# Another order for the mixers of the second block: differential maps, GLA and HGRN first, then NSA; levels later in priority

## The chip, the cores and the metric

The kernel runs on one core of a Trainium2 chip. The metric is the device time of one execution in microseconds (us), as a median of runs. The engines are PE (matrix products), DVE (vector), ACT (scalar functions), POOL (GpSimd) and SP (it issues the loads).

## The reference, cut to what matters

Two blocks of two layers each, 256 tokens, width 1024, all in float32. The change touches the attention part of the second block, which runs once a layer:

```python
for i in range(DEPTH):                      # 2 layers
    u = rms_norm_2(h, norm_attn[i]) @ w_in[i]          # 3228 columns, split
    o_a = nsa_attention(...)   # gates: compressed + selected + window attention
    o_b = diff_attention(...)  # softmax map 0 minus lambda times softmax map 1
    o_c = gla_mixer(...)       # gated linear attention, 4 heads, dk 32
    o_d = hgrn2_mixer(...)     # the same recurrence, forget gate f, 4 heads, dk 64
    h = h + jnp.concatenate([o_a, o_b, o_c, o_d], -1) @ w_out[i]
    ...                        # dense FFN (layer 0) or 8 experts (layer 1)

# NSA: hidden = silu(blocks of 32 tokens @ cmp_w1) ; kc, vc = hidden @ cmp_w2
#   o = g0 * attn(q, kc, vc) + g1 * attn(q, k_slc, v_slc) + g2 * attn(q, k_win, v_win)
# GLA and HGRN: S_t = diag(exp(log_g_t)) S_{t-1} + k_t v_t^T ;  o_t = S_t^T q_t
```

With 256 tokens every block is selected and every token lies in the window, so the selected and the window part are two causal maps with keys of their own.

## The kernel before, in words

A float32 product is computed as three products of split operands (`mm3`, lines 143 to 148: high x high, low x high, high x low). Weights are loaded 1024 rows deep by SP, split on ACT (`whi`, line 136) and DVE or POOL (`wlo`, line 139). `proj_tok` gives tokens on partitions (tile `pt`), `proj_ch` channels on partitions (tile `pc`).

Each layer runs `block2_mixers`. Its program has these parts, by the names in the profile:

- dqk projection: q and k of differential attention, squared and scaled, then transposed (`dqt`).
- nsa (512 columns) and nd (396 columns): NSA's q, k, v and gates, and the v of differential attention. From them NSA's keys and queries are normed (`nsq`, `nr`, `qn`) and transposed (`nqt`).
- `compressed()`: compressed attention of NSA, a serial chain: block sums (`zp`, `BT`), the product with cmp_w1 in two halves (`hp`, `ht`), then `kcp`, `kcs`, `kct`, `kbd`, `scp`, a softmax on 16 columns (`pcm`), `pct`, `pcT`, and `oc`.
- vr, rq, gqk: values, GLA's gate, queries, keys and forget gates. A scan along time gives the summed log gates (`gcat`), products of q and k on the diagonal give `dg`, and from it `AT` is started as a diagonal matrix.
- The levels: the decay between tokens i and j is split at seven block sizes (1 to 64). Each level computes `E` (DVE, then the exponential on ACT), `Kt` (POOL), `Qg` (DVE), two `Qh` (POOL), then the products `pg`, `ph` (PE), of which DVE (for the largest sizes ACT) copies a part into `AT`. An eighth one (`Ex`, `Ktx`, `Qgx`, `Qhx`, `pgx`, `phx`) covers the two halves of the sequence.
- The maps: softmax maps of NSA (`nl`, `npr`, `npt`, `npo`) and of differential attention (`dl`, `de`, `dpt`, `dpo`). `npt` is a transpose on PE, `nptT` its copy by ACT, and `npo` the product with the values, scaled into `mix` on DVE.
- og and rio: gates and HGRN's values, 256 and 512 columns.
- gpo (`AT` times values), the norm, the transposes of `mix` (`ptr`), and the out-projection (tiles `pt` on `xh`).

The order on each engine is made by a scheduler that simulates the program. Among the instructions that it takes to be ready it puts the one of smallest priority first; a priority is the place in the program, unless the program sets `tc.cur_priority`. Each engine then executes in that order. Before the change the program sets it three times: what follows the start of `compressed()` gets 3000 more, the rest of `compressed()` and all the maps get the smaller number back. PSUM tiles come from a pool with tags: "mx" (3 banks: maps), "gd" (2 banks: levels, `dg`, compressed attention, `gpo`) and "mm" (projections).

Of the kernel before, what the change touches and what calls it, by code (L numbers as in the profile page):

```python
# [10 lines left out]
F32 = mybir.dt.float32  # L11
# [1080 lines left out]
LEVELS = (1, 2, 4, 8, 16, 32, 64)  # L1092

# [84 lines left out]
def block2_mixers(k, a, l, hl, pre):  # L1178
# [5 lines left out]
    with ExitStack() as es:  # L1184
# [56 lines left out]
        proj_tok(k, w[:, 0:512], 512, hl, ev_n)  # L1241
        proj_tok(k, [w[:, 512:652], w[:, 1164:1420]], 396, hl, ev_nd)

        nr = one.tile([P, 2, 6], F32, name="nr")
        for tt in range(2):
            sq = n2("nsq")[:, :384].rearrange("p (g d) -> p g d", g=6)
            f = lambda s_, e_: nsa[:, tt, s_:e_].rearrange("p (g d) -> p g d", d=64)
            nc.gpsimd.tensor_tensor(sq[:, 0:4], f(0, 256), f(0, 256), op=ALU.mult)  # L1250
            nc.gpsimd.tensor_tensor(sq[:, 4:5], f(384, 448), f(384, 448), op=ALU.mult)
            nc.gpsimd.tensor_tensor(sq[:, 5:6], f(512, 576), f(512, 576), op=ALU.mult)
            nc.vector.tensor_reduce(nr[:, tt], sq, axis=AX.X, op=ALU.add)
        nrf = nr.rearrange("p t g -> p (t g)")
        nc.vector.tensor_scalar(nrf, nrf, 1.0 / 64, EPS, op0=ALU.mult, op1=ALU.add)
        powm(k, nrf, nrf, -0.5)
        qT = one.tile([P, 2, T], F32, name="nqT")
        kTs = one.tile([P, T], F32, name="nkTs")
        kTw = one.tile([P, T], F32, name="nkTw")
        for tt in range(2):  # L1260
            gain = lambda i: r2.nsa[:, 64 * i : 64 * i + 64]
            qn = n2("qn").rearrange("p (g d) -> p g d", d=64)
            for g in range(6):
                src = [0, 64, 128, 192, 384, 512][g]
                dst = qn[:, g if g < 5 else 6]
                nc.vector.scalar_tensor_tensor(dst, nsa[:, tt, src : src + 64], nr[:, tt, g : g + 1],
                                               gain(0 if g < 4 else g - 2), op0=ALU.mult, op1=ALU.mult)
            nc.gpsimd.tensor_copy(qn[:, 5], qn[:, 4])
            nc.gpsimd.tensor_copy(qn[:, 7], qn[:, 6])
            pt = pst("nqt")  # L1270
            for m in range(4):
                nc.tensor.transpose(pt[:, m * P : (m + 1) * P], qn[:, 2 * m : 2 * m + 2].rearrange("p g d -> p (g d)"),
                                    k.ident)
            sl = slice(tt * P, (tt + 1) * P)
            nc.scalar.copy(qT[:, :, sl], pt[:, :256].rearrange("p (m t) -> p m t", m=2))
            nc.scalar.copy(kTs[:, sl], pt[:, 256:384])
            nc.scalar.copy(kTw[:, sl], pt[:, 384:512])
# [5 lines left out]

        def compressed():
            zp = gdt("zp").rearrange("p (j n) -> p j n", j=4)[:, :2]
            selm = k.ident.rearrange("p (n two) -> p n two", two=2)
            for j in range(2):
                for par in range(2):
                    for tt in range(2):
                        nc.tensor.matmul(zp[64 * par : 64 * par + 64, j, tt * 64 : tt * 64 + 64],  # L1290
                                         nsa[:, tt, 256 + 64 * j : 320 + 64 * j], selm[:, :, par],
                                         start=True, stop=True)
            sel4 = one.tile([P, 32], F32, name="sel4")
            nc.vector.tensor_reduce(sel4, k.ident.rearrange("p (q n) -> p n q", q=4), axis=AX.X, op=ALU.add)
            zt = one.tile([P, 2, P], F32, name="zt")
            nc.vector.tensor_copy(zt, zp)

            BT = [n2("BT").rearrange("p (m n) -> p m n", m=16) for _ in range(2)]
            hid = one.tile([P, 2, 2, 15], F32, name="hid")
            w2c = one.tile([P, 2, 2, 64], F32, name="w2c")  # L1300
            nc.sync.dma_start(w2c, a["nsa_cmp_w2_2"][l].rearrange("j (b p) d -> p j b d", p=P))
            hr = one.tile([P, 2, 4, 16], F32, name="hr")
            nc.vector.memset(hr, 0.0)
            for j in range(2):
                nc.gpsimd.memset(BT[j], 0.0)
                z3 = zt[:, j].rearrange("p (n m) -> p n m", m=8)
                pos = k.pc[:, PC_POS + 32 * l + 16 * j : PC_POS + 32 * l + 16 * j + 16]
                for hf in range(2):
                    o = BT[j][:, 8 * hf : 8 * hf + 8, :15].rearrange("p m n -> p n m")
                    nc.vector.tensor_tensor(o, z3[:, hf : hf + 15, :],  # L1310
                                            pos[:, None, 8 * hf : 8 * hf + 8].to_broadcast([P, 15, 8]), op=ALU.add)
            yield
            for j in range(2):

                hp = gdt("hp")[:, :256]
                raws = [load_w(k, a["nsa_cmp_w1_2"][l, j, q * 1024 : (q + 1) * 1024, :], 256) for q in range(2)]
                for m in range(16):
                    nc.tensor.matmul(hp[32 * (m % 4) : 32 * (m % 4) + 32], BT[j][:, m], raws[m // 8][:, m % 8, :],
                                     start=m < 4, stop=m >= 12)
                hs = n2("chs")[:, :256]  # L1320
                nc.scalar.copy(hs, hp)
                yield

                ht = gdt("ht")[:, :32].rearrange("p (b n) -> p b n", b=2)
                for b in range(2):
                    nc.tensor.matmul(ht[:, b], hs[:, b * P : (b + 1) * P], sel4[:, :16], start=True, stop=True)
                th = n2("cth")[:, :32].rearrange("p (b n) -> p b n", b=2)
                nc.scalar.activation(th, ht, AF.Tanh, scale=0.5)
                nc.vector.scalar_tensor_tensor(th, th, 1.0, ht, op0=ALU.add, op1=ALU.mult)
                nc.vector.tensor_scalar(hid[:, j], th[:, :, :15], 0.5, None, op0=ALU.mult)  # L1330
                yield
            for b in range(2):
                nc.vector.tensor_copy(hr[:, b, :, 0:15], hid[:, 1, b : b + 1, :].to_broadcast([P, 4, 15]))
            kp = gdt("kcp")
            for b in range(2):
                nc.tensor.matmul(kp[:15, 0:64], hid[:, 0, b, :], w2c[:, 0, b, :], start=b == 0, stop=b == 1)
            for b in range(2):
                nc.tensor.matmul(kp[:64, 64:128], hr[:, b].rearrange("p h n -> p (h n)"), w2c[:, 1, b, :],
                                 start=b == 0, stop=b == 1)
            kcs = one.tile([P, 2, 64], F32, name="kcs")  # L1340
            nc.vector.memset(kcs[:16], 0.0)
            ks1 = one.tile([16, 1], F32, name="ks1")
            kj = one.tile([16, 64], F32, name="kj")
            nc.scalar.activation(kj[:15], kp[:15, 0:64], AF.Square, accum_out=ks1[:15])
            nc.vector.tensor_scalar(ks1[:15], ks1[:15], 1.0 / 64, EPS, op0=ALU.mult, op1=ALU.add)
            nc.gpsimd.tensor_tensor(ks1[:15], ks1[:15], k.pw[-0.5][:15, 0:1], op=ALU.pow)
            for j in range(2):
                nc.vector.scalar_tensor_tensor(kcs[:15, j, :], kp[:15, 0:64], ks1[:15], r2.nsa[:15, 64:128],
                                               op0=ALU.mult, op1=ALU.mult)
            vbd = one.tile([64, 4, 64], F32, name="vbd")  # L1350
            nc.vector.tensor_tensor(vbd, kp[:64, None, 64:128].to_broadcast([64, 4, 64]),
                                    c["bd16"][:64, :, None].to_broadcast([64, 4, 64]), op=ALU.mult)
            yield
            kct = gdt("kct")
            nc.tensor.transpose(kct[:, :16], kcs[:16].rearrange("p a d -> p (a d)"), k.ident[:16, :16])
            kbd = one.tile([P, 2, 16], F32, name="kbd")
            nc.vector.tensor_tensor(kbd, kct[:, None, :16].to_broadcast([P, 2, 16]),
                                    c["bd64"][:, :, None].to_broadcast([P, 2, 16]), op=ALU.mult)
            yield
            scp = gdt("scp")[:, :128].rearrange("p (t h n) -> p t h n", t=2, h=4)  # L1360
            for tt in range(2):
                for m in range(2):
                    nc.tensor.matmul(scp[:, tt, 2 * m : 2 * m + 2, :], qT[:, m, tt * P : (tt + 1) * P], kbd,
                                     start=True, stop=True)
# [762 lines left out]
```

## Time and profile before

| what | value |
| --- | --- |
| median of 3 runs | 2451.25 us (2448.11 to 2455.19) |
| profiled execution | 2451.29 us, its span 2449.2 us |
| mean granted clock of PE in the span | 0.981 |
| PE busy | 2355.3 us, 96% |
| DVE, ACT, POOL busy | 1905.5, 1469.9, 457.8 us |
| mixers of layer 0, dqk's tail to the out-projection | 722.5 to some 872 us of the span |

Times in the profile are microseconds from the span's start. A window's row gives its length, each engine's busy time with the number of instructions, the share of full clock that PE was granted, the share of the DMA engines and the rate. A timeline row joins neighbours of one form; its xN counts records, and PE's ends are modelled, so that neighbours overlap: the distance of two starts is what one costs.

### The profile page before, as it was taken

The page shows a single profiled execution, that of the slowest core. Times are in us where ns is not written, and L with a number is a line of the kernel's source. Part 1 is how long each engine was busy: PE and PEld are TensorE (multiplying, and loading weights), DVE is VectorE, ACT ScalarE, POOL GpSimd, SP SyncE. Part 2 cuts the span into 40 slices and gives each one's busy share as a digit, 9 for nine tenths or more (in the row PEclk, how much of TensorE's full clock was granted, in tenths as well). Part 3 has the DMA queues.
Part 4 walks back from the last instruction along what each step waited for, and adds up shares of the span by engine and source line. Part 5 has one row for each costly group of instructions (what it writes and reads, how often), then busy time and mean ns, then how long its engine had stood idle before and what let it go on. Part 6 is the DMA issues. An engine that isn't in the chain of part 4 may idle for free. (4 is left out here: it accounts for less than half of the span.)

```text
span 2449.2 us, 35398 instructions
## 1 busy us (share of the span) xinstructions
PE 2355.3 (96%) x13251; PEld 1972.1 (81%) x13251; DVE 1905.5 (78%) x2828; ACT 1469.9 (60%) x2239; POOL 457.8 (19%) x466
## 2 busy tenths in 40 slices
PE   8999999999999799999988999999999999999997
PEld 7898879888878589998776787887878787878785
DVE  5858576776766955556587799999999999998996
ACT  5455554455455444445454677777777777777774
POOL 3434114532133621111454100000000000000000
PEclk9999999999999799999997999999999999999999
DMA  7343254343345135465540999999999999999962
GB/s 245 105 138 121 87 168 156 122 137 121 130 158 173 39 129 196 166 206 192 160 143 5 360 367 332 355 346 342 344 345 344 342 345 343 345 343 345 344 255 87
DMA packets 288734, 550.07 MB, mean 225 GB/s; under 512 B 17414, under 2 KB 95020, under 8 KB 288300
## 3 DMA queue, kind: packets, MB, share of 16 engines
q1 hardware_dynamic: 287372, 546.67, 64.0%
q8 instruction: 106, 1.74, 0.3%
q0 software_dynamic: 144, 1.05, 0.1%
q14 instruction: 72, 0.59, 0.1%
q10 hardware_dynamic: 1040, 0.03, 0.0%
HBM read 545.61 MB, written 2.10 MB: 224 GB/s over the span
## 5 line engine op out<-in xcount | busy, mean ns | idle before, releaser
L139 DVE TENSOR_TENSOR wlo<-raw,whi 128x1024 fp32r<-128x1024 f32 x948 | 1159.9, 1240 | 294.8 <-ACT whi L136 285.8
L136 ACT CAST whi<-raw 128x1024 fp32r<-128x1024 f32 x984 | 1025.4, 1048 | 549.8 <-PE pt L147 92.1
L145 PE MATMUL pt<-whi,xh 128*128 128x512 f32 (+3 forms) x656 | 251.6, 396 | 14.6 <-DVE q L606 3.1
L146 PE MATMUL pt<-wlo,xh 128*128 128x512 f32 (+3 forms) x656 | 256.7, 392 | 2.9 <-DVE wlo L139 2.6
L147 PE MATMUL pt<-whi,xl 128*128 128x512 f32 (+3 forms) x656 | 253.2, 388 | 0.0
L237 POOL TENSOR_TENSOR nr<-nms,pwm 128x1 f32<-128x1 f32 x16 | 8.8, 549 | 1155.2 <-DVE nms L252 1155.2
L146 PE MATMUL ya<-wlo,hh 128*128 128x512 f32 x448 | 180.8, 404 | 0.0
L145 PE MATMUL mg<-whi,xg 128*128 128x512 f32 x448 | 180.4, 403 | 0.0
L146 PE MATMUL mg<-wlo,xg 128*128 128x512 f32 x448 | 178.0, 397 | 0.0
L147 PE MATMUL mg<-whi,xg 128*128 128x512 f32 x448 | 176.8, 395 | 0.0
L145 PE MATMUL mu<-whi,xg 128*128 128x512 f32 x448 | 176.8, 395 | 0.0
L146 PE MATMUL mu<-wlo,xg 128*128 128x512 f32 x448 | 176.7, 394 | 0.0
L147 PE MATMUL ya<-whi,hl 128*128 128x512 f32 x448 | 176.6, 395 | 0.0
L147 PE MATMUL mu<-whi,xg 128*128 128x512 f32 x448 | 176.6, 394 | 0.0
L145 PEld LDWEIGHTS pt<-whi,xh 128*128 128x128 f32 x656 | 125.0, 192 | 40.3 <-issue 8.8
L145 PE MATMUL pc<-xh,whi 128*128 128x256 f32 (+1 forms) x496 | 145.2, 293 | 6.5 <-DVE q L605 2.2
L146 PEld LDWEIGHTS pt<-wlo,xh 128*128 128x128 f32 x656 | 125.7, 192 | 28.9 <-DVE wlo L139 6.2
L146 PE MATMUL pc<-xl,whi 128*128 128x256 f32 (+1 forms) x496 | 143.9, 290 | 0.0
L147 PEld LDWEIGHTS pt<-whi,xl 128*128 128x128 f32 x656 | 125.6, 192 | 22.6 <-DVE xl L278 1.1
L147 PE MATMUL pc<-xh,wlo 128*128 128x256 f32 (+1 forms) x496 | 143.7, 290 | 0.0
L145 PE MATMUL ya<-whi,hh 128*128 128x512 f32 x448 | 140.8, 395 | 0.0
L145 PE MATMUL gu<-xh,whi 128*128 128x256 f32 x448 | 126.7, 283 | 0.0
(638 smaller groups left out, 4795.1 us busy)
## 6 DMA issues: line engine op xcount, KB each, us to landing
raw<-in_moe_w_gate SPq DMA_DIRECT2D x112, 1024.0 KB, 5.6
raw<-in_moe_w_up SPq DMA_DIRECT2D x112, 1024.0 KB, 5.3
raw<-in_moe_w_down SPq DMA_DIRECT2D x112, 1024.0 KB, 5.4
raw<-in_w_in SPq DMA_DIRECT2D x92, 1024.0 KB, 5.2
raw<-in_w_out SPq DMA_DIRECT2D x16, 1024.0 KB, 5.0
raw<-in_ffn_w_gate SPq DMA_DIRECT2D x14, 1024.0 KB, 5.2
raw<-in_ffn_w_up SPq DMA_DIRECT2D x14, 1024.0 KB, 5.3
raw<-in_ffn_w_down SPq DMA_DIRECT2D x14, 1024.0 KB, 5.6
```

The lines of the kernel that those rows point to most:

```text
L136: nc.scalar.copy(hi, raw_view)
L139: k.last_split = eng.tensor_sub(lo, raw_view, hi)
L145: nc.tensor.matmul(out, lh, rh, start=start, stop=False)
L146: nc.tensor.matmul(out, lh, rl, start=False, stop=False)
L147: return nc.tensor.matmul(out, ll, rh, start=False, stop=stop)
L237: return k.nc.gpsimd.tensor_tensor(out, in_, k.pw[e][:, :n], op=ALU.pow)
```

## The change

The parts of `block2_mixers` stand in another order. Differential maps come right behind the gates, alone; then vr, GLA's gate, rq, gqk, the scan, `dg` and the start of `AT`; then the nsa projection with its preparation; then `compressed()` and the NSA maps in turns; then the levels, og, rio and the rest. In place of the settings of `tc.cur_priority` there is one addition of 3000 ahead of the levels, never taken back. `compressed()` takes its PSUM tiles from "mx" instead of "gd". The first NSA product of a head is written to `mix` and the second added to it; the compressed part, which was copied there first, is added last. The functions that move are unchanged but for what is shown.

```diff
+LATER = 3000
...
-        proj_tok(k, w[:, 0:512], 512, hl, ev_n)
-        proj_tok(k, [w[:, 512:652], w[:, 1164:1420]], 396, hl, ev_nd)
+        proj_tok(k, [w[:, 512:652], w[:, 1164:1420]], 396, hl, ev_nd)
...
+        staggered([(1, tt, m) for tt in range(2) for m in range(2)], [diff_a, diff_b])
...
+        proj_tok(k, w[:, 1676:1948], 272, hl, ev_vr, kload=4, ksub=4)
...
+        proj_ch(k, w[:, 2204:2716], 512, hl, ev_rq)
+        proj_ch(k, w[:, 1420:1676], 256, hl, ev_gqk)
...
+        proj_tok(k, w[:, 0:512], 512, hl, ev_n)
...
-            zp = gdt("zp").rearrange("p (j n) -> p j n", j=4)[:, :2]
+            zp = pst("zp").rearrange("p (j n) -> p j n", j=4)[:, :2]
...
-            oc = gdt("oc")
+            oc = pst("oc")
...
-                nc.scalar.copy(mix[:, tt, O_NSA : O_NSA + 256], oc[:, tt * 256 : (tt + 1) * 256])
+                o = mix[:, tt, O_NSA : O_NSA + 256]
+                nc.vector.tensor_add(o, o, oc[:, tt * 256 : (tt + 1) * 256])
...
-                for n in range(2):
-                    nc.vector.scalar_tensor_tensor(o, po[:, n, :], su[:, n : n + 1], o, op0=ALU.mult, op1=ALU.add)
...
+                nc.vector.tensor_scalar(o, po[:, 0, :], su[:, 0:1], None, op0=ALU.mult)
+                nc.vector.scalar_tensor_tensor(o, po[:, 1, :], su[:, 1:2], o, op0=ALU.mult, op1=ALU.add)
...
-        comp = compressed()
-        next(comp)
-        first = tc.cur_priority
-        tc.cur_priority = first + 3000
...
-        last, tc.cur_priority = tc.cur_priority, first
-        for _ in comp:
-            pass
-        first, tc.cur_priority = tc.cur_priority, last
...
+        interleave(compressed(), nsa_maps())
+        tc.cur_priority += LATER
...
-        last, tc.cur_priority = tc.cur_priority, first
-        staggered([(kind, tt, m) for tt in range(2) for m in range(2) for kind in (1, 0)], [map_a, map_b])
-        tc.cur_priority = last
```

The order on PE in layer 0 shows it at two places. The first is the levels. Before, the first level's products stood among those of rio (`pt` on `xh`, 512 columns) and of a map's transpose:

```order
L1637 MATMUL pg<-Qg,Kt 128x256 x2
L1639 MATMUL ph<-Qh,Kt 128x128
L147 MATMUL pt_8968<-whi,xl 128x512
L145 MATMUL pt_8968<-whi,xh 128x512
L146 MATMUL pt_8968<-wlo,xh 128x512
L1639 MATMUL ph<-Qh,Kt 128x128
L1415 MATMUL npt<-cst,npr 128x128 x2
L1639 MATMUL ph<-Qh,Kt 128x128 x2
```

Now no projection stands in the levels. These rows are a map's transpose, the seventh level, and behind it the first products of og (`pt`, 256 columns), which rio follows:

```order
L1265 MATMUL npt<-cst,npr 128x128 x2
L1644 MATMUL pg<-Qg,Kt 128x256 x2
L1646 MATMUL ph<-Qh,Kt 128x128 x4
L145 MATMUL pt_8902<-whi,xh 128x256
L145 MATMUL pt_8903<-whi,xh 128x256
L146 MATMUL pt_8902<-wlo,xh 128x256
L147 MATMUL pt_8902<-whi,xl 128x256
```

So og and rio moved from among the levels to behind the seventh.

The second place is the end of compressed attention. Before, `oc` stood within the products of og:

```order
L147 MATMUL pt_8902<-whi,xl 128x256
L145 MATMUL pt_8902<-whi,xh 128x256
L1394 MATMUL oc<-vbd,pcT 128x256 x2
L146 MATMUL pt_8902<-wlo,xh 128x256
L147 MATMUL pt_8902<-whi,xl 128x256
```

and what stood ahead of the out-projection (`pt` with number 9133) was the last maps and single transposes of `mix`:

```order
L1708 MATMUL gpo<-vv,ATx 128x64
L1709 MATMUL gpo<-vv,AT 128x64
L275 MATMUL ptr<-cst,mix 128x128
L1448 MATMUL npo<-nsa,nptT 128x64 x4
L1415 MATMUL npt<-cst,npr 128x128 x4
L275 MATMUL ptr<-cst,mix 128x128 x4
L145 MATMUL pt_9133<-whi,xh 128x512
```

Now the last map is followed by compressed attention from `kcp` on, by all sixteen transposes, and by the out-projection:

```order
L1265 MATMUL npt<-cst,npr 128x128 x4
L1298 MATMUL npo<-nsa,nptT 128x64 x4
L1532 MATMUL kcp<-w2c,hid 15x64 x2
L1534 MATMUL kcp<-w2c,hr 64x64 x2
L1551 MATMUL kct<-cst,kcs 128x16
L1559 MATMUL scp<-kbd,nqT 128x32 x4
L1584 MATMUL pct<-cst,pcm 64x128 x2
L1590 MATMUL oc<-vbd,pcT 128x256 x2
L275 MATMUL ptr<-cst,mix 128x128 x16
L145 MATMUL pt_9133<-whi,xh 128x512
```

The chain of compressed attention moved from the middle of the projections to the last place before the out-projection.

## Rows read from the trace of the kernel before

**Rows 1.** The page's first part: busy time and share of each engine.
```profile
PE 2355.3 (96%) x13251; PEld 1972.1 (81%) x13251; DVE 1905.5 (78%) x2828; ACT 1469.9 (60%) x2239; POOL 457.8 (19%) x466
```
**Rows 2.** Layer 0 stretches: length; busy PE, PEld, DVE, ACT, POOL; PEclk, DMA, GB/s.
```profile
736.20:754.60 18.40, 17.05 (x149) 12.05 (x147) 9.99 (x36) 7.66 (x21) 6.70 (x10) 1.00 0.67 213
754.60:795.00 40.40, 39.68 (x293) 36.19 (x293) 30.18 (x77) 26.67 (x69) 13.38 (x12) 0.96 0.47 159
795.00:818.70 23.70, 18.48 (x74) 13.38 (x73) 22.54 (x28) 11.20 (x25) 20.85 (x14) 0.79 0.25 88
818.70:860.00 41.30, 30.32 (x158) 22.66 (x159) 35.37 (x76) 14.43 (x36) 20.09 (x19) 0.79 0.03 8
799.40:847.70 48.30, 36.21 (x167) 26.81 (x168) 47.73 (x81) 15.18 (x36) 35.14 (x28) 0.76 0.13 47
```
**Rows 3.** Stretches, layer 1: the levels.
```profile
1284.50:1332.00 47.50, 36.33 (x161) 27.54 (x162) 39.38 (x82) 19.49 (x49) 25.45 (x21) 0.71 0.02 6
```
**Rows 4.** PE's waits, 722 to 877: total us, times, longest.
```profile
PE pg L1637 <- DVE AT L1649: 5.8, 3, 4.9
```
**Rows 5.** PE's timeline: start us, duration us, instruction [idle before, releaser].
```profile
754.57 0.39 PE L145 MATMUL pc<-xh,whi 128*128 128x256 f32 x1 [0.69 <-ACT whi L136]
...
782.44 0.28 PE L145 MATMUL pt<-whi,xh 128*128 128x256 f32 x1
...
857.43 0.70 PE L1428 MATMUL nl<-nkTs,nqT 64*128 64x256 f32 x4
...
868.82 0.60 PE L275 MATMUL ptr<-cst,mix 128*128 128x128 f32 x4
...
870.64 0.40 PE L145 MATMUL pt<-whi,xh 128*128 128x512 f32 x1
870.87 0.39 PE L146 MATMUL pt<-wlo,xh 128*128 128x512 f32 x1
...
872.03 1.00 PE L1448 MATMUL npo<-nsa,nptT 128*128 128x64 f32 x8
...
876.07 0.50 PE L145 MATMUL pt<-whi,xh 128*128 128x512 f32 x1 [0.84 <-ACT xh L277]
```
**Rows 6.** POOL's groups, 715 to 885: total us, mean ns, idle before.
```profile
L1620 POOL TENSOR_TENSOR Kt<-kcat,E 128x768 f32<-128x768 f32 x7 | 13.7, 1959 | 9.2 <-PE ph L1639 9.2
L1630 POOL TENSOR_TENSOR Qh<-qbh,E 128x256 f32<-128x256 f32 x14 | 12.9, 940 | 0.0
...
L1598 POOL TENSOR_TENSOR AT<-cst,dg 128x1024 f32<-128x1024 f32 x2 | 4.5, 2280 | 0.0
...
L237 POOL TENSOR_TENSOR nr<-nr,pwm 128x12 f32<-128x12 f32 x1 | 2.3, 2270 | 1.1 <-DVE nr L1255 1.1
```
**Rows 7.** Timelines of ACT, DVE and PE: compressed attention's chain.
```profile
765.11 0.20 ACT L1344 ACTIVATE kj<-kcp 15x64 f32<-15x64 f32 x1
...
766.22 0.27 DVE L1348 SCALAR_TENSOR_TENSOR kcs<-kcp,ks,bc_nsag 15x64 f32<-15x64 f32 x1 [0.58 <-POOL ks L1346]
...
771.82 0.97 PE L1363 MATMUL scp<-kbd,nqT 128*128 128x32 f32 x8
...
776.61 0.35 DVE L1384 TENSOR_TENSOR pcm<-pcm,cmx 128x64 f32<-128x64 f32 x2
...
783.01 1.13 PE L1394 MATMUL oc<-vbd,pcT 64*128 64x256 f32 x4
```
**Rows 8.** The page's list of DMA issues: KB each, us to landing.
```profile
raw<-in_w_in SPq DMA_DIRECT2D x92, 1024.0 KB, 5.2
```
**Rows 9.** DVE's timeline: E beside POOL's work, and alone.
```profile
803.97 2.71 DVE L1611 TENSOR_TENSOR E<-gcat 128x384 f32<-128x384 f32 x1 [0.35 <-POOL Qh L1630]
...
837.93 0.55 DVE L1611 TENSOR_TENSOR E<-gcat 128x384 f32<-128x384 f32 x1
```
**Rows 10.** POOL's timeline: a level's Kt and Qh.
```profile
831.92 1.84 POOL L1620 TENSOR_TENSOR Kt<-kcat,E 128x768 f32<-128x768 f32 x1 [2.29 <-PE ph L1639]
833.73 1.41 POOL L1630 TENSOR_TENSOR Qh<-qbh,E 128x256 f32<-128x256 f32 x2
```

More of the change, by code (lines that the diff above doesn't have):

```diff
@@ L1240, in ev_nd @@
             nc.scalar.copy(dv[:, tt, :], ps[:, 140:396])
-        proj_tok(k, w[:, 0:512], 512, hl, ev_n)
         proj_tok(k, [w[:, 512:652], w[:, 1164:1420]], 396, hl, ev_nd)
[L1246 to L1277, printed above, removed]
         gates = one.tile([P, 2, 12], F32, name="ngate")
@@ new lines, in block2_mixers @@
+        nrf = nr.rearrange("p t g -> p (t g)")
+        nc.vector.tensor_scalar(nrf, nrf, 1.0 / 64, EPS, op0=ALU.mult, op1=ALU.add)
+        powm(k, nrf, nrf, -0.5)
+        qT = one.tile([P, 2, T], F32, name="nqT")
+        kTs = one.tile([P, T], F32, name="nkTs")
+        kTw = one.tile([P, T], F32, name="nkTw")
+        for tt in range(2):
+            gain = lambda i: r2.nsa[:, 64 * i : 64 * i + 64]
+            qn = n2("qn").rearrange("p (g d) -> p g d", d=64)
+            for g in range(6):
+                src = [0, 64, 128, 192, 384, 512][g]
+                dst = qn[:, g if g < 5 else 6]
+                nc.vector.scalar_tensor_tensor(dst, nsa[:, tt, src : src + 64], nr[:, tt, g : g + 1],
+                                               gain(0 if g < 4 else g - 2), op0=ALU.mult, op1=ALU.mult)
+            nc.gpsimd.tensor_copy(qn[:, 5], qn[:, 4])
+            nc.gpsimd.tensor_copy(qn[:, 7], qn[:, 6])
+            pt = pst("nqt")
+            for m in range(4):
+                nc.tensor.transpose(pt[:, m * P : (m + 1) * P], qn[:, 2 * m : 2 * m + 2].rearrange("p g d -> p (g d)"),
+                                    k.ident)
+            sl = slice(tt * P, (tt + 1) * P)
+            nc.scalar.copy(qT[:, :, sl], pt[:, :256].rearrange("p (m t) -> p m t", m=2))
+            nc.scalar.copy(kTs[:, sl], pt[:, 256:384])
+            nc.scalar.copy(kTw[:, sl], pt[:, 384:512])
@@ L1602, in block2_mixers, with nsa_maps @@
+        def nsa_maps():
+            before = None
+            for it in [(0, tt, m) for tt in range(2) for m in range(2)] + [None]:
+                now = it and (nsa_a(*it), it)
+                if before:
+                    nsa_b(before[0], *before[1])
+                before = now
+                yield
+        interleave(compressed(), nsa_maps())
+        tc.cur_priority += LATER
         AX_ = one.tile([P, 8, P], F32, name="ATx")
@@ L1677, in block2_mixers @@
         nc.scalar.copy(AX_[:, 4:8, :], ph)
-        last, tc.cur_priority = tc.cur_priority, first
-        def map_a(kind, tt, m):
-            return (nsa_a, diff_a)[kind](kind, tt, m)
-        def map_b(r, kind, tt, m):
-            return (nsa_b, diff_b)[kind](r, kind, tt, m)
-        staggered([(kind, tt, m) for tt in range(2) for m in range(2) for kind in (1, 0)], [map_a, map_b])
-        tc.cur_priority = last
         def silu2(out, ps, n):
```

224 lines of the change are left out of this document (116 added, 108 removed).

## The prediction

> **What bounds the kernel now.** I read the page's first part, then the stretches of layer 0's mixers, then PE's waits there, then the timelines of PE and POOL. PE is busy 96% of the span [rows 1], so the end moves only if PE idles more or less than now; what is moved but hidden behind PE is worth nothing. The stretches show where it idles [rows 2]: in the projections (754.6 to 795.0) PE is busy 39.68 of 40.40 us, but from 795.0 to 818.7 and 818.7 to 860.0 only 18.48 of 23.70 and 30.32 of 41.30, at a granted clock of 0.79, while DVE is busy 22.54 and 35.37. That is the stretch of the seven levels (pg, ph). Layer 1 shows the same: 36.33 busy of 47.50, clock 0.71 [rows 3]. The waits name what ends last [rows 4]: pg waits for DVE's copies into AT, 5.8 us in three waits, 4.9 the longest. So the mixers, some 150 us a layer, are bound at their end by the chains level -> DVE -> POOL -> PE and softmax -> transpose -> output, with projections beside them to fill PE. Both layers are priced from layer 0: the program is the same, and the levels' stretch alike.
>
> **The path before.** I count from the end of the dqk projection's tail (722.5) to the out-projection. Its products come 0.23 us apart (870.64, 870.87), and the 19th starts at 876.07 [rows 5], so without the work between them the first would start at 876.07 - 18 x 0.23 = 871.9. Before: 149.4 us. Inside lie rq and gqk, 754.57 to 782.44, 27.9 us; then og and rio (0.23 us for 512 columns, half of it for 256; 48 products each: 11.0 + 5.5), which stand among the maps and the first levels; then the last maps, 857.43 to the end of 872.03's npo, 15.6 us.
>
> **The path after, part by part.** The order of PE says which work stands alone now.
> - nd and nsa change places. Of nd's 48 products 36 stand in dqk's tail, 12 remain: 2.3 us (396/512 x 0.23 = 0.18 each). nsa comes later, beside the scan and dg: 48 x 0.23 = 11.0, plus some 2 for dg's products and the first level's E, Kt, Qh: 13.
> - vr with the first differential maps: the stretch 736.20 to 754.60 took 18.40 with NSA's preparation, hp and the first maps [rows 2]. Without hp and nqt I take 14.
> - rq and gqk with the other differential maps: 27.9 as before; the maps that stood there (NSA's) had the same shape.
> - Levels. PE holds levels 1 to 5 back to back and og, rio only behind level 7. In POOL's queue the levels now stand with the NSA preparation: Kt 13.7, Qh 12.9, AT 4.5, the power for nr 2.3 [rows 6], and by their sizes some 5.7 of squares, copies and BT: 39. With PE's 2 for the last level: 41. Before, first Kt to last Kt took 48.3 [rows 2], but with og's rest, rio, and maps inside. The gain of taking DVE's splits and maps away is in those 7 us. Bounds: 33, if the operations ran at their shortest; 50, if DVE and POOL exclude each other (rivals).
> - og, rio and what is left of the first NSA maps: 16.5 for the products, 3 for pgx and phx, 3 for two nl, 4 for npt and npo: 27 (24 to 31). This work was half hidden in the levels; here it is bare.
> - Last maps and gpo: 15.6 as before, plus hp of the second half, ht and one more trip npt -> ACT -> npo: 19 (16 to 22).
> - Compressed attention. Before, oc stood among og's products, hidden. After, kcp, kct, scp, pct, oc follow on PE with nothing between. From kj to the end of kcs: 765.11 to 766.49, 1.4. kct and kbd have no row near; 1.0 by kcs's 0.27 and a transpose. From scp to pcm's end: 771.82 to 776.96, 5.1. pct and its copy 1.0, oc 1.13 [rows 7], two additions to mix 0.8 (an estimate by kcs, four times as wide). Sum 10.5. Bounds: 5, if its first half ends beside the last maps; 14, if it waits for the three "mx" banks it now shares with the maps. Nothing else is queued behind oc but the transposes of mix.
> - Transposes of mix: all 16 behind oc, where before 15 stood among other products: 4 x 0.60 and one wait of 0.84 for ACT [rows 5], 3.5 with some at the lower clock.
>
> Sum: 2.3 + 14 + 27.9 + 13 + 41 + 27 + 19 + 10.5 + 3.5 = 158.2. Less 149.4: 8.8 a layer. I take 8.4, since nd's shorter products end dqk's tail a little earlier: 16.8 for two layers.
>
> What costs nothing: two ACT table loads fewer a layer, as ACT is not waited for in that stretch; the first NSA product as a tensor_scalar instead of an accumulation, same DVE time; LATER, since all that follows carries it as well and it reorders nothing against work already issued. SP's queue holds cmp_w1 before og, and with four weight buffers og's load waits for hp's first half. That stands before level 6, two levels of 41/7 us ahead of og, 11.7 us. A load takes 5.2 us to land [rows 8], and the split behind it on ACT and DVE some 2.5 (an estimate from Kt's 768 columns on POOL): 7.7, hidden by 4 us, and 3 to 5 us a layer dearer if hp comes late.
>
> The profiled run took 2451.29 us, span 2449.2, the median of the runs is 2451.25: no correction. 2451.3 + 16.8 = 2468.
>
> **A rule weighed.** DVE's E took 2.71 us at 803.97, with POOL in a split and then AT, and 0.55 at 837.93, with POOL idle [rows 9]; so DVE and POOL do hold each other up here. The Trainium skill, "SBUF — State Buffer", Who interferes with whom, says that a DVE instruction with two SBUF inputs contends with a GpSimd instruction that reads SBUF, and that whoever comes first holds the shared ports for the whole instruction. By it a level is a plain sum over both engines, and the trace agrees for E. That sum is the second rival below.
>
> **Rivals.**
> 1. Faster. The levels now have banks of their own and DVE has neither splits nor differential maps in that stretch. If E runs at 0.55 instead of 2.71, Kt at 1.84 and a pair of Qh at the 1.41 of a quiet stretch [rows 10], seven levels are 22.8 on POOL, with some 10 to 11 of other POOL work 33: 8 less than in my sum, and if half of the bare compressed chain also ends beside the last maps (5 less), a layer is 4 shorter than before: 2451 - 8 = 2443. It decides when the levels take under 34 us. For it: the 4.9-us wait of pg for AT, which the maps on DVE caused. Against it: POOL's 39 is a sum of busy times, and its queue also takes NSA's preparation in. 0.2.
> 2. Slower still. DVE and POOL alternate: E 1.1 (two at 0.55), Kt 1.96, two Qh 1.88, Qg 0.7 (by E's 384 columns) are 5.6 a level, 39 for seven, with AT, nr and the rest 50. Then 9 more a layer: 2486. For it: the two E [rows 9]. Against it: before, POOL was busy 35.14 of 48.30 and DVE 47.73 [rows 2], and a blocked instruction counts as busy, so the rows don't tell how much of it was blocking; the levels' shares alone (POOL 26.6 of Kt and Qh) leave DVE room. 0.2.
> 3. No change. og and rio run while POOL is late only in the scheduler's list, and PE's idle time merely moves: what the levels lose as cover the maps win. 2451. 0.15.
> 4. My forecast, 2468, with its own range 2459 to 2478. 0.45.
>
> **Numbers.** A measurement of this kernel tells 0.3% (7.4 us) from no change. Faster by more: 0.19, nearly all of rival 1. Same: 0.17, rival 3 and a little of either neighbour. Slower: 0.64. Range 2438 to 2488: from rival 1 with one us more a layer, to rival 2.
>
> **What would show it.** Right: in the profile after, PE's busy share in the levels falls (under half) and its clock too; og's first product starts right after the seventh ph; behind the last npo stand some 10 us in which PE runs fewer than 30 matmuls, waiting for DVE and ACT in the compressed chain; vr to rq and gqk take what they took. Each layer 6 to 11 us longer between dqk's tail and the out-projection. Wrong: levels under 34 us, or the compressed chain ended before the last maps, or og standing between levels.

## The result, and the profile after

The changed kernel took 2495.7 us (2482.7 to 2498.0), the kernel before 2450.1 in runs on the same chip: a ratio of 1.0169, interval 1.0153 to 1.0185. The ratio goes by means, and one of the four runs, at a clock of 0.974 against 0.967 to 0.968, took 2482.7: the loss is 41 us by the ratio. By the medians it is 46 against these runs and 44 against the 2451.3 of the table above; I use 45 below. The direction was forecast; the size was not: 17 were predicted, and the time lies above the range's end of 2488.

The profiled run's span is 2496.3 us, 47.1 longer than before. This is the first part of its page, which answers to [rows 1]:

```profile
PE 2370.5 (95%) x13251; PEld 1986.1 (80%) x13251; DVE 1915.0 (77%) x2832; ACT 1465.1 (59%) x2231; POOL 452.1 (18%) x466
```

PE issues the same 13251 instructions and is busy 15.2 us longer, so about a third of the 47.1 us is the same work taking longer, which I put down to the lower clock (0.967 against 0.981), and two thirds is idle time.

The stretches of layer 0 answer to [rows 2]. They run from the first `dqt` to the out-projection; the columns are as there. First fine:

```profile
720.60:736.20 15.60, 14.87 (x99) 12.25 (x97) 8.63 (x20) 10.60 (x33) 4.92 (x3) 0.93 0.79 264
736.20:761.80 25.60, 25.60 (x195) 23.91 (x195) 16.82 (x43) 15.44 (x34) 6.42 (x4) 0.91 0.26 84
761.80:777.30 15.50, 13.97 (x70) 10.94 (x68) 14.96 (x27) 8.60 (x13) 10.90 (x12) 1.00 0.36 109
777.30:812.00 34.70, 19.83 (x84) 15.63 (x84) 33.04 (x51) 5.44 (x8) 31.98 (x31) 0.56 0.04 12
812.00:828.00 16.00, 12.39 (x83) 8.33 (x83) 11.53 (x30) 8.90 (x30) 7.96 (x9) 0.79 0.39 132
828.00:853.30 25.30, 25.30 (x150) 20.87 (x150) 13.96 (x29) 13.08 (x29) 6.16 (x4) 1.00 0.38 130
853.30:872.10 18.80, 16.72 (x141) 13.37 (x139) 10.53 (x31) 7.58 (x19) 4.74 (x4) 0.96 0.36 121
872.10:883.80 11.70, 6.00 (x23) 4.08 (x23) 4.28 (x21) 0.98 (x4) 0.54 (x1) 0.50 0.00 0
883.80:887.20 3.40, 3.37 (x17) 3.38 (x17) 1.69 (x3) 1.69 (x3) 0.00 (x0) 0.50 0.00 0
```

Then the levels in one row, and the sum over the path (its means are over four stretches).

```profile
777.30:828.00 50.70, 32.22 (x167) 23.97 (x167) 44.58 (x80) 14.34 (x37) 39.94 (x39) 0.63 0.15 50
...
sum 166.60, PE 138.06 PEld 112.75 DVE 115.44 ACT 72.30 POOL 73.62; mean PE 34.51 PEld 28.19 DVE 28.86 ACT 18.08 POOL 18.41
```

The row to look at is the fourth: in 34.70 us DVE and POOL are busy nearly throughout, and PE for 19.83 us, at 0.56 of full clock. Before, the same path took 149.4 us, and a window over it reads:

```profile
722.50:871.90 149.40, 130.91 (x847) 107.45 (x846) 110.23 (x243) 73.31 (x174) 72.69 (x65) 0.90 0.32 105
```

So layer 0 is 17.2 us longer: PE idles 28.5 us where it idled 18.5 (10), and nearly the same instructions (851 records in one window over the stretch, 847 before) are busy 138.1 us where they took 130.9 (7). Of the two levels of the clock, 1.2 and 2.4 GHz, the last two rows of the first table stand at the lower (0.50) and the levels' first row close to it (0.56): both are stretches in which PE had run short, dependent groups with gaps between.

Layer 1 repeats it. The row that answers to [rows 3]:

```profile
1273.60:1324.80 51.20, 29.26 (x169) 21.76 (x168) 44.80 (x81) 11.63 (x29) 38.10 (x38) 0.70 0.12 41
```

The router's first product behind the mixers of layer 1 (PE's timeline, in the profile before and after) marks the end of all that the change touches:

```profile
1374.16 0.28 PE L145 MATMUL lt<-xh,rs 128*8 128x256 f32 x1 [1.23 <-ACT xh L277]
```

```profile
1415.05 0.28 PE L145 MATMUL lt<-xh,rs 128*8 128x256 f32 x1 [1.23 <-ACT xh L277]
```

By then 40.9 us are lost: 15.3 up to layer 0's out-projection (17.2, less 1.9 by an earlier start), 3.8 before layer 1's first `dqt`, 21.3 in its mixers (171.9 against 150.6), and 0.5 behind them. The experts behind it took 1081.2 us against 1075.0. The change doesn't touch them, and in the twelve other kernels below they took 1076 to 1079, so these 6 us of the 47 have no cause that I can name.

**What makes the levels long.** These are rows of POOL's timeline there (start, duration, instruction, in brackets the idle time before it and its releaser):

```profile
788.49 1.82 POOL L1627 TENSOR_TENSOR Kt<-kcat,E 128x768 f32<-128x768 f32 x1
...
795.64 2.26 POOL L237 TENSOR_TENSOR nr<-nr,pwm 128x12 f32<-128x12 f32 x1
...
809.88 1.81 POOL L1627 TENSOR_TENSOR Kt<-kcat,E 128x768 f32<-128x768 f32 x1 [2.36 <-ACT E L1625]
...
816.90 1.82 POOL L1627 TENSOR_TENSOR Kt<-kcat,E 128x768 f32<-128x768 f32 x1 [2.31 <-ACT E L1623]
...
824.05 0.99 POOL L1671 TENSOR_TENSOR Ktx<-kcat,Ex 128x384 f32<-128x384 f32 x1 [5.33 <-PE ph L1646]
```

POOL waits 10.0 us in three places (2.36, 2.31 and 5.33); its other waits there are under a microsecond. The first two are for `E`. DVE's timeline says why it is late: NSA's norm and the block sums stand ahead of it in the queue.

```profile
799.20 0.90 DVE L1618 TENSOR_TENSOR E<-gcat 128x384 f32<-128x384 f32 x1
800.02 1.07 DVE L1620 TENSOR_TENSOR E<-gcat 128x384 f32<-128x384 f32 x1
801.02 0.75 DVE L1656 COPY_PREDICATED AT<-lvm,ph 128x256 f32<-128x256 uint32 x2
801.68 4.97 DVE L1467 SCALAR_TENSOR_TENSOR qn<-nsa,nr,bc_nsag 128x64 f32<-128x64 f32 x12
...
807.83 0.54 DVE L1618 TENSOR_TENSOR E<-gcat 128x384 f32<-128x384 f32 x1
...
810.15 3.94 DVE L1506 TENSOR_TENSOR BT<-zt,pc 128x120 f32<-128x120 f32 x4
```

The third is for PE, which had compressed attention's `hp` and the first maps ahead of the sixth level, at half clock, and POOL needs that level's buffer back for `Ktx`. It is not POOL that the seventh level waits for: its `Kt` is done at 818.72 and its `pg` starts at 826.27, behind `hp`, the sixth level and a pair of maps. PE's timeline goes on to the end of the path:

```profile
790.37 2.08 PE L1644 MATMUL pg<-Qg,Kt 128*128 128x256 f32 x4 [6.40 <-POOL Kt L1627]
...
811.36 0.60 PE L1473 MATMUL nqt<-cst,qn 128*128 128x128 f32 x4
...
817.47 3.64 PE L1514 MATMUL hp<-raw,BT 128*32 128x256 f32 x32 [3.24 <-ACT nkTw L1478]
821.04 1.97 PE L1644 MATMUL pg<-Qg,Kt 128*128 128x256 f32 x4
...
827.14 1.05 PE L1646 MATMUL ph<-Qh,Kt 128*128 128x128 f32 x8
827.95 0.48 PE L145 MATMUL pt<-whi,xh 128*128 128x256 f32 x2
...
870.32 1.77 PE L1298 MATMUL npo<-nsa,nptT 128*128 128x64 f32 x8 [0.73 <-ACT nptT L1267]
872.02 0.61 PE L1532 MATMUL kcp<-w2c,hid 128*15 128x64 f32 x4
872.56 0.69 PE L1534 MATMUL kcp<-w2c,hr 128*64 128x64 f32 x4
875.03 0.26 PE L1551 MATMUL kct<-cst,kcs 16*128 16x16 f32 x1 [1.78 <-DVE kcs L1544]
875.57 1.92 PE L1559 MATMUL scp<-kbd,nqT 128*128 128x32 f32 x8 [0.28 <-DVE kbd L1553]
880.18 0.61 PE L1584 MATMUL pct<-cst,pcm 128*64 128x128 f32 x2 [2.70 <-DVE pcm L1580]
881.24 2.07 PE L1590 MATMUL oc<-vbd,pcT 64*128 64x256 f32 x4 [0.45 <-ACT pcT L1586]
883.83 3.67 PE L275 MATMUL ptr<-cst,mix 128*128 128x128 f32 x16 [0.52 <-DVE mix L1594]
887.15 0.70 PE L145 MATMUL pt<-whi,xh 128*128 128x512 f32 x1
```

The row of `hp` has a wait of 3.24 us for ACT's `nkTw`. `hp` doesn't read `nkTw`; that copy is the last to read `nqt`, which stands on "mx" as `hp` now does, so what `hp` waited for is probably the bank, which I infer and no run isolates.

So NSA's projection ends at 777.3, but `nqt`, the transposes of its normed queries and keys, only at 812.0: its squares, the power for `nr`, `qn` and the copies each queue up behind a level's work. All NSA maps, then the rest of compressed attention, then all sixteen `ptr` follow one another from there. That chain ends last.

### The profile page after: what moved, and what is told of

The parts are those of the page before. It is cut to its first block, busy times and chain, and to the rows that moved or that the text cites. A ratio compares the mean times of both kernels' runs of the same rounds, so it can differ in the third digit from the quotient of the medians.

```text
span 2496.3 us, 35390 instructions
## 1 busy us (share of the span) xinstructions
PE 2370.5 (95%) x13251; PEld 1986.1 (80%) x13251; DVE 1915.0 (77%) x2832; ACT 1465.1 (59%) x2231; POOL 452.1 (18%) x466
## 5 line engine op out<-in xcount | busy, mean ns | idle before, releaser
L136 ACT CAST whi<-raw 128x1024 fp32r<-128x1024 f32 (+1 forms) x984 | 1025.4, 1048 | 558.6 <-PE pt L147 97.3
L146 PEld LDWEIGHTS pt<-wlo,xh 128*128 128x128 f32 x656 | 127.0, 194 | 35.1 <-DVE wlo L139 11.8
```

The source lines that it names most:

```text
L136: nc.scalar.copy(hi, raw_view)
L146: nc.tensor.matmul(out, lh, rl, start=False, stop=False)
```

## Experiments

All ratios are to the kernel before, run on the same chip as the kernel in question, with three rounds each; times are medians. The kernels start from the changed one unless said otherwise. Where an expectation means no change, it counts from 2491 us, some 5 below the median above.

**Gates among the levels** (gates_loaded_early). Is the path long because PE lacks og and rio there? The weights of both are loaded earlier, so that their products can run between the levels, as before.

```diff
+        graws = list(loads(k, w[:, 1948:2204], 256, kload=8))
+        rraws = list(loads(k, w[:, 2716:3228], 512))
         interleave(compressed(), nsa_maps())
...
-        proj_tok(k, w[:, 2716:3228], 512, hl, ev_rio)
+        proj_tok(k, None, 512, hl, ev_rio, pre=chunks(k, None, 512, raws=rraws))
```

> The changed kernel, with the loads of og's and rio's weights issued ahead of compressed attention's cmp_w1 (nothing else moved by hand). In the order on PE og and rio now stand among the first three levels. Theory A (cmp_w1 holds the weight buffers until hp, so og and rio can't fill PE in the levels): their 25 us behind level 7 shrink to the maps' 9, the levels grow by some 5, so 10 to 12 us a layer less: 2467 to 2473. Theory B (the levels are bound by DVE and POOL, with NSA's preparation in their queues, and PE has nothing to do with it): the six splits, 5 on DVE at 1.2 and one on POOL at 2.4 us, lengthen the levels by 8 a layer, so only 6 to 8 a layer less: 2475 to 2480. In both the levels' stretch is longer than the 51 us of the changed kernel.

Measured: 2500.9, ratio 1.0197 (1.0175 to 1.0219). Both expectations missed. og and rio do run among the levels, and the 16.5 us behind them are gone, yet PE's timeline ends where it did:

```profile
870.63 1.70 PE L1298 MATMUL npo<-nsa,nptT 128*128 128x64 f32 x7
...
881.48 2.07 PE L1590 MATMUL oc<-vbd,pcT 64*128 64x256 f32 x4 [0.45 <-ACT pcT L1586]
```

Two things cancel: without og and rio it is 52.5 us from the last `nqt` to the last `npo` instead of 60.1, but with their splits in the queues of the levels the last `nqt` is done at 819.8 instead of 812.0. So work of PE taken from behind the levels gains nothing where NSA's chain starts later by as much.

**NSA's preparation back in its place** (nsa_prep_first). The nsa projection, norms and transposes stand behind dqk again; the rest of the change stays.

```diff
+        proj_tok(k, w[:, 0:512], 512, hl, ev_n)
         proj_tok(k, [w[:, 512:652], w[:, 1164:1420]], 396, hl, ev_nd)
+        nr = one.tile([P, 2, 6], F32, name="nr")
...
-        proj_tok(k, w[:, 0:512], 512, hl, ev_n)
```

> The changed kernel, with the nsa projection and its norm and transposes back behind dqk, as before the change. Theory A: hp comes with the second level, og and rio stand among levels 4 to 7, 8 to 12 us a layer less. Theory B: DVE's qn (5.0) and nr, POOL's nsq (3), nr (2.3) and copies (1.7) leave the levels, whose stretch falls from 51 to some 42: 9 us a layer less, beside A's. If both hold, 17 to 20 a layer: 2451 to 2457. If only one, 2471 to 2475.

Measured: 2470.5, 1.0075 (1.0058 to 1.0092): 25 of the 45 us come back, by this part alone, about what was expected if only one theory holds. But theory B's shorter levels didn't come: on PE they last from 788.7 to 839.3, 50.6 us, where the changed kernel has 780.2 to 828.2, 48.0. They are no shorter without `qn`, `nr` and `nsq` in the queues; og, much of rio and three pairs of maps now stand among them, and PE is busy 45.8 of the 50.6 us. The compressed steps are still bare before the out-projection, which starts at 878.9.

**Compressed attention wholly ahead of the NSA maps** (compressed_first).

```diff
-        interleave(compressed(), nsa_maps())
+        for _ in compressed():
+            pass
+        for _ in nsa_maps():
+            pass
```

> The changed kernel, with compressed attention wholly ahead of the NSA maps in the program, its result copied into mix first and the maps added to it, as before the change. The order on PE puts kcp to oc among rio's products and leaves the maps last. If the bare chain (11.8 us behind the last map in layer 0) is what it seems, it goes; but the maps then have no projection beside them, some 19 us become 24 to 27. 4 to 8 us a layer less than the changed kernel: 2475 to 2483. If the chain is only exchanged for the maps' own waits: 2491.

Measured: 2496.7, 1.0188 (1.0171 to 1.0205), no gain, nearer to the second expectation. `oc` is written at 847 instead of 883, but now the last maps end at 885, beside the first products of the out-projection only. The two only changed places: what stands last waits on other engines, whichever it is.

**Two steps of compressed attention for each pair of maps** (two_steps).

```diff
-        interleave(compressed(), nsa_maps())
+        comp = compressed()
+        for _ in nsa_maps():
+            for _ in range(2):
+                next(comp, None)
+        for _ in comp:
+            pass
```

> The changed kernel, with two steps of compressed attention behind each NSA map pair instead of one, so that kcp, kct and scp stand among the last maps. Theory C (the mixers end on NSA's own chain: preparation queued among the levels, then four pairs of maps, then compressed attention's last steps bare): the bare part falls from 11.8 to some 5 us, 4 to 8 us a layer less: 2477 to 2485. Theory D (the levels' 51 us are the bound, what follows is PE's work alone): no change, 2491.

Measured: 2490.8, 1.0158 (1.0141 to 1.0175). The interval overlaps the change's (1.0153 to 1.0185), so no gain is shown, and theory C's 8 to 16 us are missed. In layer 0 the path takes 166.5 us, as in the changed kernel.

**Preparation and compressed attention both early** (prep_compressed_first). The NSA preparation behind dqk, and compressed attention interleaved with the differential maps, its tiles still on "mx".

```diff
-        staggered([(1, tt, m) for tt in range(2) for m in range(2)], [diff_a, diff_b])
...
+        interleave(compressed(), diff_maps())
...
-        interleave(compressed(), nsa_maps())
```

> The changed kernel, with the nsa projection and its preparation behind dqk and with compressed attention in turns with the differential maps, early (its result copied into mix first, as before the change). NSA's maps, the levels, og and rio stay as in the change. Theory C: both the late preparation and the bare end are gone, 17 to 24 us a layer less than the changed kernel: 2443 to 2457. Theory D: as with the preparation alone, 2468 to 2473, since the levels still take some 50 us.

Measured: 2479.7, 1.0116 (1.0099 to 1.0133), a miss for both, and 9 slower than with the preparation alone. Something in the early compressed chain costs more than its better place brings. The banks were the suspect, so the next kernel takes this one line of the change alone.

**Only the banks** (before_banks: the kernel *before* with one edit).

```diff
-            zp = gdt("zp").rearrange("p (j n) -> p j n", j=4)[:, :2]
+            zp = pst("zp").rearrange("p (j n) -> p j n", j=4)[:, :2]
...
-            oc = gdt("oc")
+            oc = pst("oc")
```

> The kernel before, with one edit: compressed attention's PSUM tiles on the maps' three banks, so that the levels have their two banks alone. The banks' part of the change by itself. Both theories: within 6 us of 2451; if the levels were held up by sharing their banks, 4 to 10 us less; if the maps are held up by the new sharing, as much more.

Measured: 2489.0, 1.0160 (1.0140 to 1.0181): 38 us for eight tile names, outside everything that was expected. PE's timeline of this kernel, and of the kernel before:

```profile
782.19 1.13 PE L1394 MATMUL oc<-vbd,pcT 64*128 64x256 f32 x4
783.25 0.49 PE L1464 MATMUL dl<-dT 32*128 32x128 f32 x4
```

```profile
744.68 0.48 PE L1464 MATMUL dl<-dT 32*128 32x128 f32 x2
```

No differential map starts before `oc` has been written; before, the first started 38.6 us earlier. The maps stand behind compressed attention in the program, and with one set of banks for both they get one only after the whole chain has had its turns, though that chain is serial. In this kernel compressed attention is ahead of the maps in priority too, so whether another priority would change the turns is not shown.

**Early compressed attention on the old banks** (early_on_gd: prep_compressed_first with the eight names back on "gd").

```diff
-            oc = pst("oc")
+            oc = gdt("oc")
```

> The version with the nsa projection, its preparation and compressed attention early, beside the differential maps (2480 us), with one edit: compressed attention's PSUM tiles back on the levels' two banks, as before the change. It is the change's order without its banks. Theory E (lockstep on the maps' banks): the differential maps run free of compressed attention, and 10 to 15 us a layer go: 2450 to 2460. If the levels are held up by sharing their banks with compressed attention: 2480 or more.

Measured: 2465.0, 1.0047 (1.0028 to 1.0066), 15 us less than on "mx" by the medians and 17 by the ratios (this chip's kernel before took 2454.7). It lies between the two expectations, nearer to theory E. Layer 0 takes 151.9 us against 149.4 before. With preparation, compressed chain and banks put back, some 11 us (0.47%) are left for the rest of the change.

**The change on the old banks** (compressed_on_gd), the same edit made in the changed kernel itself.

```diff
-            zp = pst("zp").rearrange("p (j n) -> p j n", j=4)[:, :2]
+            zp = gdt("zp").rearrange("p (j n) -> p j n", j=4)[:, :2]
...
-            oc = pst("oc")
+            oc = gdt("oc")
```

> The changed kernel, with compressed attention's PSUM tiles back on the two banks of the levels. In the order on PE all levels now stand behind oc, at the end, with nothing beside them. If banks of their own are what lets the levels start early, the seven levels stand bare at some 35 to 40 us a layer and the maps ahead of them overlap with og and rio: 10 to 25 us a layer more, 2510 to 2540. If the banks don't matter: 2491.

Measured: 2508.0, 1.0233 (1.0216 to 1.0250), just below what was expected. In the change's own order the levels stand behind compressed attention, and on one set of banks all of them wait for `oc`. Then they run with nothing beside them, and a window shows how long seven take without NSA in their queues:

```profile
861.00:889.00 28.00, 22.03 (x86) 17.13 (x87) 24.45 (x39) 5.57 (x11) 20.94 (x16) 0.68 0.00 1
```

28 us for the seven levels on PE, where the changed kernel has 48.0. Part of the difference is that the first operands were ready here; the rest, as I take it, is the other work in the changed kernel's stretch. The bank move that costs 38 us in the old order gains 12 in the new one, by the medians.

**The projections' banks** (compressed_on_mm): three banks that neither maps nor levels use.

```diff
-            oc = pst("oc")
+            oc = k.pmm.tile([P, 512], F32, tag="mm", name="oc")
```

> The changed kernel, with compressed attention's PSUM tiles on the projections' three banks, which stand empty between the nsa and the og projection. The banks are taken in the program's order, so on the maps' banks each map waits for the step of compressed attention ahead of it (theory E: that lockstep makes NSA's chain long), and here it doesn't; og and rio in turn wait for oc. Theory E: from the last nqt to the last npo 60 us become 40 to 45, oc comes 15 to 20 us sooner, og and rio then stand bare behind it (17 us): within 6 us a layer of the changed kernel in total, 2480 to 2500, but with oc before 870 in layer 0 (883 in the changed kernel). Without lockstep as a cause (theory C alone: late preparation): oc stays at 878 or later and og and rio add 17 us a layer: 2515 to 2530.

Measured: 2512.0, 1.0243 (1.0226 to 1.0260), between the two expectations; theory E's two signs in the trace came true (`oc` before 870, and the 44.7 us below), its time did not. The maps no longer take turns with compressed attention, and `oc` comes 23 us earlier, 3 of them by an earlier start:

```profile
804.85 3.50 PE L1514 MATMUL hp<-raw,BT 128*32 128x256 f32 x32 [0.69 <-DVE BT L1506]
...
857.85 2.07 PE L1590 MATMUL oc<-vbd,pcT 64*128 64x256 f32 x4 [0.46 <-ACT pcT L1586]
```

But og and rio now wait for a bank until then and stand bare behind it, to 878.5; the out-projection starts at 887.6. From the last `nqt` to the last `npo` it is 44.7 us here and 52.5 with the gates among the levels. That is not yet the price of the turns on "mx": 16.0 us of the 52.5 are the rest of the levels, and 7.3 of the 44.7. From the end of the seventh level, behind which neither has og or rio until `oc`, it is 37.4 us here and 36.5 there to the end of the last `npo`, and 41.9 and 47.7 to the end of `oc`; I put the price of the turns at some 6 us, an estimate from these two. The levels changed as well: `hp` waits 0.69 us, for `BT`, which it reads, instead of 3.24 for `nkTw`, and the seven levels take 42.2 us in layer 0 (775.9 to 818.1) instead of 48.0. In layer 1 they take 51.2 against 50.4, so that this gain is not one to count on.

**Qh on DVE** (qh_on_dve). If DVE and POOL shut each other out, as in rival 2, it is the sum of the two that counts, and moving work from POOL to DVE costs nothing; if they are two queues, the longer one decides.

```diff
-                nc.gpsimd.tensor_tensor(bs4(Qh[:, cb]), od4(k.qbh[:, cb]), bc4(od(E[:, 1 + cb, :]), 2),
+                nc.vector.tensor_tensor(bs4(Qh[:, cb]), od4(k.qbh[:, cb]), bc4(od(E[:, 1 + cb, :]), 2),
```

> The changed kernel, with Qh computed on DVE instead of POOL. If DVE and POOL exclude each other in the levels (the second rival), 13 us of POOL become some 5 of DVE, and the levels fall by 5 to 8 a layer: 2475 to 2482. If they run side by side and DVE's queue is the longer one (NSA's qn, BT and nr stand in it), the levels grow by 3 to 5 a layer: 2497 to 2502.

Measured: 2506.3, 1.0222 (1.0205 to 1.0240), 11 slower than the change and above both expectations. A window over most of its levels, and PE's waits (total us, times, longest):

```profile
779.00:812.00 33.00, 17.14 (x76) 13.27 (x76) 32.76 (x57) 5.62 (x13) 20.58 (x19) 0.59 0.02 6
```

```profile
PE pg L1644 <- DVE AT L1656: 14.4, 4, 10.4
```

DVE is full and POOL is not. Over all seven levels, first here and then in the changed kernel:

```profile
781.30:828.00 46.70, 30.73 (x159) 23.58 (x160) 44.37 (x88) 12.69 (x32) 24.43 (x19) 0.65 0.13 46
```

```profile
780.20:828.20 48.00, 32.42 (x168) 24.15 (x169) 41.84 (x78) 13.95 (x38) 37.24 (x37) 0.63 0.13 44
```

The busy time of DVE and POOL together falls from 79.1 to 68.8 us, and the levels by 1.3. So they don't follow the sum; they don't grow with DVE's share either, as they should by the other expectation. The 11 us are lost behind the levels: from there to the first `ptr` it is 63.9 us (828.0 to 891.9), where the changed kernel has 55.7 (828.2 to 883.9). PE is busy 54.0 us of them instead of 47.9, at a clock of 0.79 against 0.88; why the clock was lower there is open.

**Levels ahead of NSA** (levels_before_nsa). The levels' code stands ahead of the nsa projection, without `LATER`: in every queue a ready level goes first.

```diff
+        AX_ = one.tile([P, 8, P], F32, name="ATx")
+        for s in LEVELS:
...
         proj_tok(k, w[:, 0:512], 512, hl, ev_n)
...
-        tc.cur_priority += LATER
```

> The changed kernel with the levels' code placed in the program ahead of the NSA projection, its preparation and the interleaved steps, and without their low priority, so that every engine takes a level's instruction before NSA's when both are ready. Theory E (the end is NSA's own chain: projection, norms, transposes, four pairs of maps, last compressed steps; the levels only hold it up): pushing the levels further ahead of it gains nothing, 2485 to 2500 us. Rival (the levels' own length decides, because VectorE and GpSimd take NSA's work between the levels' instructions): the levels take 36 to 41 us instead of 51 in each layer and the time falls to 2465 to 2478 us.

Measured: 2506.4, 1.0213 (1.0192 to 1.0234), 6 above what was expected. The levels don't get shorter: on PE they last from 781.8 to 831.7, 49.9 us, where the changed kernel has 48.0, and POOL waits 7.7 us for the sixth one's `ph`, since `hp` stands ahead of it on PE all the same. Priority in the program chooses only between instructions that are ready together; it takes none out of the queue.

**The maps' order alone** (before_diff_first: the kernel *before*, its differential maps first, in place, at the same priority and on the same banks).

```diff
-        staggered([(kind, tt, m) for tt in range(2) for m in range(2) for kind in (1, 0)], [map_a, map_b])
+        staggered([(kind, tt, m) for kind in (1, 0) for tt in range(2) for m in range(2)], [map_a, map_b])
```

> The kernel before with one part of the change alone: in its staggered maps all pairs of differential heads come first and the NSA pairs after them; place, priority and banks stay. Theory E (the maps' order by itself costs nothing as long as the compressed chain runs beside them on banks of its own): within 6 us of the kernel before, 2445 to 2457 us. Rival (the NSA maps late make the last NSA output late, as in the changed kernel): 2460 us or more.

Measured: 2445.7, 0.9978 (0.9968 to 0.9987), as expected. The one part of the change that gains by itself: 5 us, less than 0.3% but with an interval that leaves 1 out. Layer 0's path:

```profile
720.90:867.40 146.50, 132.31 (x847) 108.74 (x846) 109.74 (x244) 73.06 (x174) 75.11 (x65) 0.90 0.33 107
```

It is 2.9 us shorter than before, with 14.2 us of PE idle instead of 18.5. It beats both kernels.

## Why the prediction was right in direction and wrong in size

Layer 0, term by term, in us:

| term of the sum | predicted | measured |
| --- | --- | --- |
| rest of nd, vr with differential maps | 16.3 | 15.6 |
| rq, gqk | 27.9 | 25.6 |
| nsa beside scan and dg | 13 | 15.5 |
| levels | 41 | 50.7 |
| og, rio, first NSA maps | 27 | 25.3 |
| last maps, gpo | 19 | 18.8 |
| compressed attention to mix | 10.5 | 11.7 |
| transposes | 3.5 | 3.4 |
| sum | 158.2 | 166.6 |

**The step that failed is the levels' term.** It was the sum of POOL's busy time, 39, and 2 for PE. The busy time was right: 39.94. Wrong was to take a sum of busy times for the length of a queue. POOL idled 10.8 us, because NSA's `qn` and `BT` on DVE stood ahead of two `E`, and `hp` on PE ahead of the sixth level. The prediction had NSA's preparation in POOL's queue as work, but not on DVE as delay; it had `hp` ahead of level 6 for og's load, but not for the level itself; and the upper bound of 50 was tied to another mechanism. The excess is 9.7 us in layer 0 and, against the same 41, 10.2 in layer 1 (51.2): some 20 of the 28 us by which the loss exceeds the forecast. The rows show where the levels waited; that they would be short without the preparation is not shown. In compressed_on_gd, bare and with their operands ready, they run in 28, but in nsa_prep_first, with the preparation gone and other work among them, in 50.6.

The sum also had no term for the lower clock, whose fall it named as a sign; it is 7 of layer 0's 17 us. Two of its small sums are off without effect: 12 times 0.18 is 2.2 and not 2.3, and rival 2's parts add up to some 52 and not 50.

**Rival 2 had nearly the size, and its mechanism only in part.** It gave 50 us for the levels and 2486 in all. DVE's `E` is indeed longer beside POOL's Kt and Qh: 0.90 and 1.07 at 799.20, against 0.54 at 807.83 with POOL idle. The Trainium skill, "SBUF — State Buffer", Who interferes with whom, has a DVE instruction with two SBUF inputs contend with a GpSimd instruction that reads SBUF; these rows agree. That one holds the other for a whole instruction they don't show. Over the stretch it is more than these rows: the 13 `E` of the seven levels take 11.3 us and the 7 `Qg` 8.9, where 0.54 and 0.68 each, as in rows with POOL idle, would make 11.8; so some 8 us of DVE's time, an estimate from these rows, come with POOL's company and lengthen the queue that `E` stands in. But the levels are not the sum of the two engines: in qh_on_dve that sum falls by 10 us and the levels by 1.3.

**What stands behind the path was seen only in part.** The prediction priced og and rio as bare and expected them to cost what they lost as cover. They are bare for 25 us, but gates_loaded_early took them away and gained nothing, since NSA's chain started 8 us later by it. The path through the mixers is NSA's own chain, from its projection through `nqt`, four pairs of maps and the last compressed steps to `ptr`. Shown is that putting its start back gives 25 us, and that exchanging its last two parts gives none. That the maps and compressed attention share three banks was taken as a possible 3.5 us (the 14 in the bounds of 10.5). By itself the move costs 38 us in the old order and 15 to 17 with an early compressed chain, and is a gain of 12 in the change's own order. These parts don't add up to 45; each depends on where the others stand.

**What was right.** og follows the seventh `ph` directly (827.95). Behind the last `npo` 23 matmuls run in 11.7 us, at the waits that were named: `kct` 1.78, `pct` 2.70. All sixteen `ptr` take 3.4. PE's busy share in the levels fell only to 64% where under half was expected, but to 57% in their first row, and the clock with it. The load of og is issued at 819.5, while the first `hp` reads cmp_w1, and is hidden, as costed. Rival 1 (levels under 34) and rival 3 (no change) are refuted.

**Left open.** Layer 1 loses 4 us more than layer 0 in the same stretch and another 3.8 ahead of it, where 36 of nd's narrower products fill dqk's tail; PE waits there for `wlo` and `dqk`, and I didn't follow it further. With everything that the experiments name put back (early_on_gd), some 11 us remain, of which no run tells the parts. The change with `LATER` left out and nothing else moved was not run.

## What to carry to other kernels

A sum of one engine's busy times is a lower bound for a stretch, not its length: when a second chain moves into the stretch, go through the queue of every engine and ask which instruction of it stands ahead of the one that the first chain waits for. Tiles that shared a rotating set of banks were served in the order of the program here (in before_banks the first map waited 38.6 us for a serial chain's last turn), so two chains that share one can be tied together; price such an edit by itself before it is buried in a reordering. And test the parts alone: here one of them gains 0.2% while the whole loses 1.7%. And a run's time doesn't tell what became of the stretch that was suspected: nsa_prep_first was faster with longer levels, qh_on_dve slower with shorter ones.

## What the runs showed that I had not expected

- PE ran the levels' first 34.7 us at 0.56 of full clock and the compressed steps at 0.50, where the levels before, with projections among them, stood at 0.76 to 0.79 [rows 2]. The lower clock is 7 of layer 0's 17 us, as I read it: nearly the same instructions, 138.1 us instead of 130.9. `oc` took 2.07 us instead of 1.13 [rows 7], the first half of `hp` 3.64 against 1.93 for the second, which stood behind projections.
- The runs of the changed kernel lie 15 us apart, where ten of the fastest kernel lie within 4 (2443.5 to 2447.6): the one at 2482.7 had the higher mean clock.
